# A list scheduler's two assumptions: half a microsecond more before TensorE's steps, and a later landing of short-row transfers

## The chip, the cores and the metric

The kernel runs on one core of one Trainium2 chip. The metric is the device time of one execution in microseconds (us). The engines are named as in the profile: PE is TensorE (PEld its weight loads), DVE is VectorE, ACT is ScalarE, POOL is GpSimd, SP is SyncE, which here only issues transfers.

## The reference, cut to what is computed

One layer of a hybrid backbone, in float32: 512 latent tokens and 256 context tokens of width 1024. A conditioning vector gives shifts, scales and gates; one wide projection feeds two groups of heads, a Mamba-2 scan (SSD) and a gated delta rule (GDN), each in both directions; then an output projection and an MLP of width 4096.

```python
p_lat = modulate(rmsnorm(x, norm1_g[l]), sh1, sc1) @ w_in[l]
p_ctx = modulate(rmsnorm(ctx, norm1_g[l]), sh1c, sc1c) @ w_in[l]
y_lat, y_ctx = token_mixers(p_lat, p_ctx, ...)      # convolutions, SSD scan, GDN scan, both directions
x = x + g1 * (y_lat @ w_out[l])
x = x + g2 * sq_relu_mlp(modulate(rmsnorm(x, norm2_g[l]), sh2, sc2), w_mlp1[l], w_mlp2[l])
...
# in gdn_scan, per chunk of 64 tokens and head:
tmat = eye + strictly_lower((k_beta k^T) * decay)
sol = triangular_solve(tmat, rhs, lower=True, unit_diagonal=True)
v_new = u_i - w_i S;   S_next = S * d_i + kd_i^T v_new;   o = qd_i S + qk_i v_new
```

The kernel inverts the triangular matrices in blocks of 128 tokens and applies the inverses in the scan.

## The kernel before, in words

Every large product is made of three PE passes over a high and a low part of both operands (`hH`, `hL`, `wH`, `wL`). The kernel runs in these stages:

- 0 to about 50 us: loads, norms and the modulation (`mp`, `xtp`), and the first weights.
- about 50 to 436 us: the projections of the items k, q, v, g, B, C, and the first x and z (`proj`, PSUM tiles `pl_*` of 512 latent columns and `pc_*` of 256 context columns, 24 passes each), each followed by a convolution on DVE (`conv`, tiles `cy_*`) and by transposes (`k3t`, `v4t` and the like). Among them run four inverses (`inverse(b)`, two heads each): `kk` and `qk` products, diagonal blocks sent to DRAM and back in another layout (`blkD` to `ND` and `YD`), a substitution on DVE (`TD`, `YD`, 60 steps), the result sent to DRAM (`invD`) and read back in blocks of 32 by 32 by 14 transfers of 48 KB with rows of 128 bytes (`X`, `Yf`, `Yb`), then small PE products (`z`, `x`, `y`, each with an ACT copy behind it), and the inverse is stored to `invF`.
- about 436 to 646 us: four scans (`scan(b)`: `ks`, `pp`, `up`, `op`), which begin by loading `Ys` from `invF`. The rest of the x and z projections and the SSD products (`st`, `yp`) lie between their steps.
- from about 680 us: output projection (`wo0a`, `wo1a`), then the MLP (`m1p`, `m2a`).

The order of instructions on each engine is not the order of the program text. `kernel()` traces the program once; `_plan` builds a graph of its instructions and dependencies (`_Graph`), gives each a cost (`_cost`), and runs an event simulation with a list of ready instructions for each engine (`run`). The order that comes out is then fixed for every engine, SP's transfers included, by `_keep`. At run time each engine follows its list strictly and waits at semaphores, so the plan's times count for nothing, but its order does.

Two places of the plan matter here. In `_cost`, a transfer occupies the queue for `gap` and lands `d` + 2000 ns after it; for an `X`, `Yf` or `Yb` load of 49,152 bytes this is 49152/150 = 328 ns of queue, and a landing 623 + 2000 = 2.6 us after that. Its issue occupies SP for 370 ns. In `run`, `finish` hands the result of instruction k to its user m on engine q:

```python
t = end + (50 if self.dma[k] else _LAT[e][q]) + _SLACK[q]
```

with `_SLACK = (0.0, 100.0, 100.0, 100.0, 0.0)`: a user on DVE, ACT or POOL gets 100 ns of margin, a user on PE (q = 0) gets none. Among ready instructions the one with the lowest `key` (mostly the place in the program text) goes first. A transfer is also held back while eight earlier ones have not landed in the plan (`_LANES`).

Of the kernel before, what the change touches and what calls it, by code (L numbers as in the profile page):

```python
# [1394 lines left out]
_WINDOW = 3413.4  # L1395
_SLACK = (0.0, 100.0, 100.0, 100.0, 0.0)
_LANES = 8
_MIX = 1.2e9
_STRETCH = 1.0

# [12 lines left out]
class _Graph:  # L1413
    def __init__(self, nc, tc, traced, ordered):
        kind = {i.name: type(i).__name__ for i in ordered}
        meta = {n for n, k in kind.items() if k.startswith("BassTile")}
        slots = {n for n in meta if kind[n] == "BassTileRelease"}
        self.ins = [i for i in traced if not kind[i.name].startswith("BassTile") and kind[i.name] != "InstRegisterMove"]
        self.at = {i.name: k for k, i in enumerate(self.ins)}
        psum, pool_of = set(), {}  # L1420
        for t in tc.tiles:
            if "PSUM" in str(t.space):
                psum.add(t.name)
        memo = {}

        def expand(n):
            if n not in memo:
                memo[n] = set()
                out = set()
                for a, _ in nc.dependency_edges(n):  # L1430
                    out |= expand(a) if a in meta else {a}
                memo[n] = out
            return memo[n]

        deps, sync, users = [], [], {}
        tiles = {t.name: t for t in tc.tiles}
        for k, i in enumerate(self.ins):
            d, s = set(), set()
            for a, info in nc.dependency_edges(i.name):
                if a in slots:  # L1440
                    continue
                if a in meta:
                    d |= expand(a)
                    s |= {x for x in expand(a) if kind[x] == "InstDMACopy"}
                else:
                    d.add(a)
                    if "NoSync" not in str(info.class_):
                        s.add(a)
            deps.append({self.at[a] for a in d if a in self.at})
            sync.append({self.at[a] for a in s if a in self.at})  # L1450
            for t in {_name(ap) for ap in list(i.outs) + list(i.ins)}:
                if t in tiles:
                    users.setdefault(t, []).append(k)
        opened = {}
        for i in traced:
            if kind[i.name] == "BassTilePoolBoundary" and "op=alloc" in str(i):
                pool = str(i).split("pool=")[1].split()[0]
                opened[pool] = {self.at[a] for a in expand(i.name) if a in self.at}
        tags = {}
        for t in tc.tiles:  # L1460
            if t.name in users:
                tags.setdefault(t.tag, []).append(t)
        for line in tags.values():
            bufs = line[0].tag_meta.bufs
            for k, t in enumerate(line):
                u = set(users[t.name])
                before = opened.get(t.mls.memorylocations[0].ant_tile_pool_name, set())
                if k >= bufs:
                    before = before | set(users[line[k - bufs].name])
                for n in users[t.name]:  # L1470
                    if not deps[n] & u:
                        deps[n] |= before
                        sync[n] |= {x for x in before if kind[self.ins[x].name] == "InstDMACopy"}
        n = len(self.ins)
        self.n, self.succ, self.need = n, [[] for _ in range(n)], [0] * n
        self.eng, self.dma, self.dur, self.gap = [], [], [], []
        self.table, self.accum, self.lock, self.shape = [], [], [], []
        for i in self.ins:
            e = _ENG.index(str(i.engine).split(".")[1])
            self.eng.append(e)  # L1480
            self.dma.append(kind[i.name] == "InstDMACopy")
            self._cost(i, e, kind[i.name], psum)
        for m in range(n):
            deps[m].discard(m)
            self.need[m] = len(deps[m])
            for d in deps[m]:
                same = self.eng[d] == self.eng[m] and not (self.dma[d] and d in sync[m])
                self.succ[d].append((m, same, d in sync[m]))

    def _cost(self, i, e, kind, psum):  # L1490
        table, accum, lock, shape = 0, False, False, 0
        w = _width(i.outs[0])
        gap = None
        if kind == "InstDMACopy":
            src = _name(i.ins[0])
            b = 4
            for q in i.outs[0].ap:
                b *= q[1]
            run = 4 * min(i.ins[0].ap[-1][1], i.outs[0].ap[-1][1])
            same = any(q[0] == 0 and q[1] > 1 for q in i.ins[0].ap)  # L1500
            gap = b / (380.0 if same else 400.0 if run >= 2048 else 320.0 if run >= 512 else 60.0 if src.startswith("in_") else 150.0)
            total = b / (300.0 if src.startswith("in_") else 140.0) + 600.0
            d = max(0.0, total - gap)
        elif e == 0:
            shape = tuple(i.tile_size)
            full = str(i.ins[0].dtype).endswith("float32") and str(i.ins[1].dtype).endswith("float32")
            if i.is_transpose:
                gap = max(84.0, 20 + 0.7 * w)
            elif not full:
                gap = 15 + 0.415 * w  # L1510
            elif shape == (32, 32):
                gap = 34.0
            elif shape[1] < 128:
                gap = 5 + 1.7 * w
            else:
                gap = max(218.0, 5 + 1.7 * w)
            d = gap + 163.0
            shape = (shape, tuple(i.tile_position or ()), full and not i.is_transpose)
        else:
            sp = [a for a in i.ins if hasattr(a, "memref") and _width(a) > 1]  # L1520
            ps = any(_name(a) in psum for a in sp)
            two = len(sp) > 1
            if e == 1:
                lock = not ps and kind != "InstMemset"
                if kind == "InstTensorTensor":
                    d = 145 + 1.04 * w
                elif kind == "InstReciprocal":
                    d = 150 + 6.2 * w
                elif kind == "InstTensorCopy":
                    d = 150 + (1.04 if ps or w >= 1024 else 0.55) * w  # L1530
                elif kind == "InstMemset":
                    d = 130 + 0.5 * w
                else:
                    d = 205 + 1.04 * w if two or ps else 140 + 0.6 * w
            elif e == 2:
                table = _TABLE.get(str(i.func).split(".")[-1], 0)
                accum = len(i.outs) > 1
                one = sum(hasattr(a, "memref") for a in i.ins) == 1
                d = (190 if one else 250) + 0.82 * w + (20 if ps else 0)
            else:  # L1540
                lock = True
                d = 250 + 2.0 * w if kind == "InstTensorTensor" else (130 if kind != "InstMemset" else 90) + 0.95 * w
        self.dur.append(d if e == 0 or gap is not None else d * _STRETCH)
        self.gap.append(gap)
        self.table.append(table)
        self.accum.append(accum)
        self.lock.append(lock)
        self.shape.append(shape)

    def run(self, key):  # L1550
# [15 lines left out]
        def finish(k, e, end, fr):  # L1566
            free[e] = fr
            heapq.heappush(events, (fr, 0, e))
            for m, same, sy in succ[k]:
                q = eng[m]  # L1570
                if same:
                    t = fr
                    if not self.dma[k] and e:
                        if self.dma[m]:
                            t = end + 28
                        elif sy:
                            t = end + (122 if self.accum[k] else 34)
                else:
                    t = end + (50 if self.dma[k] else _LAT[e][q]) + _SLACK[q]
                if t > ready[m]:  # L1580
                    ready[m] = t
                need[m] -= 1
# [5 lines left out]
        while done < n:  # L1588
# [15 lines left out]
            if not now[e]:  # L1604
                if soon[e]:
                    heapq.heappush(events, (soon[e][0][0], 0, e))
                continue
            p, k = heapq.heappop(now[e])
            if self.dma[k] and len(landed) >= _LANES and landed[-_LANES] > t:
                heapq.heappush(soon[e], (landed[-_LANES] + 30.0, p, k))  # L1610
                heapq.heappush(events, (t, 0, e))
# [73 lines left out]
def _plan(trace):  # L1685
# [12 lines left out]
    graph = _Graph(nc, tc, traced, ordered)  # L1698
    rank = graph.rank()
    key = [_MIX * k / graph.n - rank[k] for k in range(graph.n)]  # L1700
    _, order = graph.run(key)
    return [[graph.ins[k].name for k in line] for line in order]

# [41 lines left out]
```

## Time and profile before

| | us |
|---|---|
| median of 3 runs | 1163.1 (1160.6 to 1168.05) |
| profiled execution, its own time | 1160.29 |
| its span, first to last instruction | 1158.6 |
| PE busy | 1091.5 (94%) |
| DVE, ACT, POOL busy | 721.4, 604.0, 456.0 |

The profiled execution took 1160.29 us, 1.7 us more than its span and 2.8 us less than the median of the runs. PE's mean granted clock was 0.978 of full speed. Busy is the time in which an engine ran an instruction. In rows of busy time by stretch the engines stand in the order PE, PEld, DVE, ACT, POOL, each with its number of instructions, behind the stretch and its length. Idle time of an engine is put down to what released it last; "issue" stands where the profile shows no release.

### The profile page before, as it was taken

Reading aid. Unit: us, or ns where it says so; the run is one execution under the profiler, and the core shown is the slowest. Engines: PE = TensorE matmul, PEld = TensorE weight load, DVE = VectorE, ACT = ScalarE, POOL = GpSimd, SP = SyncE. Lnnn points to the kernel's source line nnn. Section 1 sums busy time; section 2 is a strip of 40 time slices with the busy share of each in tenths; the row PEclk is TensorE's granted clock in tenths of the full one; section 3 lists DMA queues with packets and bytes.
Section 4 is the critical chain, followed back from the end, with each engine's and each line's share of the span. In section 5 each row is a group of like instructions: output and inputs, shape, how many; then the busy total and the mean of one; then the engine's idle time right before and its main releaser. Section 6 shows DMA issues by size and latency. Waiting matters only on the chain.

```text
span 1158.6 us, 19228 instructions
## 1 busy us (share of the span) xinstructions
PE 1091.5 (94%) x7120; PEld 885.4 (76%) x7120; DVE 721.4 (62%) x1402; ACT 604.0 (52%) x1419; POOL 456.0 (39%) x386
## 2 busy tenths in 40 slices
PE   5799998998989999999999989999999999999997
PEld 2458877787868777788878868777777888888885
DVE  3775699897979557578766777878673022444023
ACT  4647656648364577578886674125333122444133
POOL 1216444442331332222322254433545445555462
PEclk9899999999999999999999989998999999999999
DMA  9577746686564694745372277743443333333332
GB/s 313 182 198 200 229 146 185 195 227 170 157 163 146 154 347 104 267 123 207 103 273 73 92 282 237 227 136 100 137 146 109 92 107 93 91 103 98 91 104 96
DMA packets 189334, 188.44 MB, mean 163 GB/s; under 512 B 41548, under 2 KB 140153, under 8 KB 189241
## 3 DMA queue, kind: packets, MB, share of 16 engines
q1 hardware_dynamic: 188336, 186.04, 52.6%
q8 instruction: 56, 0.92, 0.3%
q10 hardware_dynamic: 905, 1.18, 0.3%
q14 instruction: 37, 0.30, 0.1%
HBM read 151.45 MB, written 35.73 MB: 162 GB/s over the span
## 4 chain that ended last, share of the span: by engine, by line
PE 70%; DVE 11%; ACT 8%; DMA 6%; issue 3%; SPq 1%; POOL 0%; ACTq 0%; DVEq 0%; POOLq 0%
PE m1p L62 15%; PE m2a L62 15%; PE wo0a L62 4%; PE wo1a L62 3%; PE pl_x L62 3%; PE pl_v L62 3%; PE pl_g L62 2%; PE yp L62 2%; PE op L62 2%; PE pc_v L62 2%; DMA st_q<-in_w_in_dram 2%; PE pp L62 2%; PE pl_z L62 2%; PE up L62 2%; PE pc_x L62 2%
## 5 line engine op out<-in xcount | busy, mean ns | idle before, releaser
L77 POOL TENSOR_TENSOR wL_m<-st_m,wH_m 128x512 fp32r<-128x512 f32 x128 | 177.4, 1405 | 186.6 <-ACT wH_m L68 177.1
L68 ACT ACTIVATE wH_m<-st_m 128x512 fp32r<-128x512 f32 x128 | 77.1, 625 | 187.0 <-PE m2a L62 111.0
L62 PE MATMUL m1p<-h2hL,wH_m 128*128 128x512 f32 (+1 forms) x272 | 104.5, 384 | 1.6 <-DVE h2hL L77 1.5
L62 PE MATMUL m1p<-h2hH,wH_m 128*128 128x512 f32 (+1 forms) x272 | 103.6, 383 | 2.5 <-ACT rl L68 2.0
L62 PE MATMUL m1p<-h2hH,wL_m 128*128 128x512 f32 (+1 forms) x272 | 103.1, 380 | 0.0
L62 PE MATMUL m2a<-wL_m,aH 128*128 128x512 f32 x256 | 99.4, 389 | 0.0
L62 PE MATMUL m2a<-wH_m,aL 128*128 128x512 f32 x256 | 99.4, 389 | 0.0
L62 PE MATMUL m2a<-wH_m,aH 128*128 128x512 f32 x256 | 98.9, 389 | 0.0
L77 DVE TENSOR_TENSOR rtmp<-m2a,g2r 128x512 f32<-128x512 f32 x16 | 10.7, 683 | 140.1 <-PE m2a L62 140.0
L77 DVE TENSOR_TENSOR rl<-rl 128x512 f32<-128x512 f32 x32 | 47.5, 1484 | 51.8 <-ACT rl L68 51.5
L62 PEld LDWEIGHTS m1p<-h2hH,wH_m 128*128 128x128 f32 x272 | 51.8, 191 | 14.0 <-ACT rl L68 4.0
L77 POOL TENSOR_TENSOR wL_wo<-st_wo,wH_wo 128x512 fp32r<-128x512 f32 x32 | 45.2, 1433 | 41.1 <-ACT wH_wo L68 35.4
L74 DVE SCALAR_TENSOR_TENSOR macc<-mw,sil,macc 128x256 f32<-128x256 f32 x84 | 56.4, 671 | 7.2 <-DMA mw<-in_w_mod_dram 5.4
L62 PEld LDWEIGHTS m1p<-h2hL,wH_m 128*128 128x128 f32 x272 | 52.1, 191 | 11.5 <-DVE h2hL L77 2.4
L77 DVE TENSOR_TENSOR TD<-YD,ND 112x30 f32<-112x30 f32 (+14 forms) x120 | 59.6, 497 | 0.9
L62 PEld LDWEIGHTS m1p<-h2hH,wL_m 128*128 128x128 f32 x272 | 52.2, 192 | 9.4
L62 PEld LDWEIGHTS m2a<-wH_m,aH 128*128 128x128 f32 x256 | 48.0, 188 | 10.1
L62 PEld LDWEIGHTS m2a<-wL_m,aH 128*128 128x128 f32 x256 | 48.0, 188 | 10.0
L62 PEld LDWEIGHTS m2a<-wH_m,aL 128*128 128x128 f32 x256 | 48.0, 188 | 9.9
L77 DVE TENSOR_TENSOR YD<-YD,TD 112x30 f32<-112x30 f32 (+14 forms) x120 | 54.5, 454 | 0.9
L665 POOL TENSOR_SCALAR_AFFINE_SELECT rw<-rw 128x512 f32<-128x512 f32 x32 | 24.0, 764 | 64.7 <-ACT er L68 60.6
L68 ACT ACTIVATE wH_wo<-st_wo 128x512 fp32r<-128x512 f32 x32 | 18.5, 623 | 50.0 <-PE wo0a L62 21.6
(496 smaller groups left out, 3224.2 us busy)
## 6 DMA issues: line engine op xcount, KB each, us to landing
st_m<-in_w_mlp_dram SPq DMA_DIRECT2D x64, 512.0 KB
wm<-in_w_mod_dram SPq DMA_DIRECT2D x16, 512.0 KB
rw<-rowsD SPq DMA_DIRECT2D x16, 512.0 KB
st_wo<-in_w_out_dram SPq DMA_DIRECT2D x16, 512.0 KB
mw<-in_w_mod_dram SPq DMA_DIRECT2D x16, 512.0 KB
Ys<-invF SPq DMA_DIRECT2D x8, 768.0 KB
st_k<-in_w_in_dram SPq DMA_DIRECT2D x8, 512.0 KB
st_g<-in_w_in_dram SPq DMA_DIRECT2D x8, 512.0 KB
```

The lines of the kernel that those rows point to most:

```text
L62: PE.matmul(o, lhsT=lhsT, rhs=rhs, start=start, stop=stop)
L68: ACT.activation(out=o, in_=i, func=f, **kw)
L74: (eng or DVE).scalar_tensor_tensor(out=o, in0=a, scalar=s, in1=b, op0=op0, op1=op1)
L77: (eng or DVE).tensor_tensor(out=o, in0=a, in1=b, op=op)
L665: POOL.affine_select(out=rw[:, d_], in_=rw[:, d_], pattern=[[0, n], [pat, P]], compare_op=ALU.is_ge, fill=NEG, base=0, channel_multiplier=cm_)
```

## The change

Two constants of the plan become active. `_EARLY = 500.0`: for every user on PE that stands in the program text before the first load of `Ys` (index `self.scans`), a result of another engine or a transfer counts as ready 500 ns later. `_SHORT = 2500.0`: a transfer that does not read an input of the kernel, and whose contiguous run is below 512 bytes, lands 2.5 us later in the plan. These are the four writes of `blkD` and the 14 loads of `X`, `Yf` and `Yb` of each inverse, and the two small `mod2` loads in the tail. The loads of `ND` and `YD` have long rows and keep their cost. The other three constants are 0 and change nothing. No instruction is added or removed and no cost on the chip changes; what changes is the order in each engine's list, everywhere behind the first choice that falls out another way.

```diff
+_SHORT = 2500.0
+_FROM = 0.0
+_EARLY = 500.0
+_LATE = 0
+_NEAR = 0.0
...
+        self.scans = min(k for k, i in enumerate(self.ins) if _name(i.outs[0]).startswith("Ys"))
...
-            d = max(0.0, total - gap)
+            d = max(0.0, total - gap) + (0.0 if src.startswith("in_") else _SHORT if run < 512 else _FROM)
...
                     t = end + (50 if self.dma[k] else _LAT[e][q]) + _SLACK[q]
+                    if q == 0 and m < self.scans:
+                        t += _EARLY
...
             p, k = heapq.heappop(now[e])
+            if e == 0 and shape and self.shape[k][0] != shape[0] and _NEAR:
...
+    rows = [k for k in range(graph.n) if graph.dma[k] and _name(graph.ins[k].ins[0]) == "in_w_mod_dram"]
+    for k in rows[24:40]:
+        key[k] += _LATE * _MIX / graph.n
```

## Rows read from the trace of the kernel before

**Rows 1.** The page, part 1: busy us (share of the span) xinstructions.

```profile
PE 1091.5 (94%) x7120; PEld 885.4 (76%) x7120; DVE 721.4 (62%) x1402; ACT 604.0 (52%) x1419; POOL 456.0 (39%) x386
```

**Rows 2.** Busy time by stretch, five engines; then PE clock, DMA share, GB/s.

```profile
0.00:50.00 50.00, 31.86 (x217) 15.81 (x218) 24.83 (x56) 27.53 (x45) 9.22 (x26) 0.90 0.74 250
50.00:436.00 386.00, 359.78 (x3170) 296.57 (x3169) 299.41 (x615) 228.68 (x535) 146.85 (x133) 0.97 0.67 194
436.00:700.00 264.00, 253.84 (x1750) 211.13 (x1750) 186.47 (x451) 195.81 (x566) 80.73 (x69) 0.99 0.50 168
700.00:1158.60 458.60, 446.04 (x1988) 361.92 (x1986) 210.68 (x283) 151.96 (x275) 219.22 (x158) 0.99 0.41 124
...
900.00:1000.00 100.00, 100.00 (x443) 82.81 (x442) 21.02 (x23) 25.73 (x45) 49.13 (x37) 1.00 0.34 100
```

**Rows 3.** Waits of PE, 50 to 436 us: total us, times, longest us.

```profile
PE y L62 <- issue: 7.0, 4, 3.8
PE z L62 <- DMA X<-invD: 4.4, 2, 2.4
PE pc_k L62 <- DVE cy_k L74: 2.6, 1, 2.6
PE k3t L65 <- DVE kT L74: 2.5, 1, 2.5
PE v4t L65 <- DVE vT L74: 1.7, 1, 1.7
PE kk L62 <- DVE At L74: 1.4, 1, 1.4
...
PE pl_v L62 <- POOL wL_v L77: 0.2, 1, 0.2
PE k1t L65 <- DVE kT L74: 0.2, 1, 0.2
```

**Rows 4.** Timeline of PE around three waits: start us, us, instruction, [idle before].

```profile
150.02 0.88 PE L65 MATMUL k3t<-ident,kT 128*128 128x128 f32 x6 [2.51 <-DVE kT L74]
150.65 0.67 PE L62 MATMUL pl_g<-hL,wH_g 128*128 128x512 f32 x1
...
272.40 0.25 PE L62 MATMUL z<-X,At 32*32 32x32 f32 x4 [2.40 <-DMA X<-invD]
272.58 0.50 PE L62 MATMUL pl_v<-hH,wH_v 128*128 128x512 f32 x1
...
395.89 0.25 PE L62 MATMUL z<-X,At 32*32 32x32 f32 x4 [2.01 <-DMA X<-invD]
396.07 0.38 PE L62 MATMUL pc_x<-hH,wL_x 128*128 128x256 f32 x1
```

**Rows 5.** Busy time in the stretches that follow four waits (columns as rows 2).

```profile
150.80:154.20 3.40, 3.40 (x10) 2.63 (x10) 3.40 (x5) 3.30 (x15) 3.00 (x3) 0.50 0.34 121
273.70:277.10 3.40, 3.40 (x17) 3.23 (x16) 3.37 (x9) 2.82 (x9) 0.00 (x0) 0.50 0.83 227
341.90:348.80 6.90, 5.82 (x59) 4.56 (x61) 2.25 (x6) 3.42 (x7) 0.00 (x0) 0.51 0.18 61
396.50:399.90 3.40, 3.40 (x18) 3.11 (x17) 0.70 (x1) 0.00 (x0) 0.00 (x0) 0.51 0.51 83
```

**Rows 6.** Timeline of SP's queue: loads of two inverses.

```profile
264.82 6.43 SPq L90 DMA_DIRECT2D X<-invD  x6
...
272.32 0.47 SPq L90 DMA_DIRECT2D Yf<-invD  x1
...
390.61 4.83 SPq L90 DMA_DIRECT2D X<-invD  x6
```

**Rows 7.** Timeline of PE: the longest wait put down to issue.

```profile
342.98 0.26 PE L62 MATMUL y<-Yf,Z 32*32 32x32 f32 x1 [3.79 <-issue]
```

**Rows 8.** DMA queues, 339 to 344 us: packets, MB, share of 16 engines.

```profile
q8 instruction: 1, 0.02, 1.3%
```

**Rows 9.** Instructions by tile: ns min/median/max, first and last start.

```profile
L62 PE MATMUL pp<-r,Ys x160: 270/275/377, 444.4 to 645.2; 128*128 128x128 f32 x160
L62 PE MATMUL pl_z<-hH,wH_z x64: 388/395/483, 417.9 to 676.2; 128*128 128x512 f32 x64
L62 PE MATMUL yp<-rw,xt x128: 272/273/421, 424.3 to 690.2; 128*64 128x128 f32 x128
```

**Rows 10.** Busy time in the stretch behind the last scan (columns as rows 2).

```profile
650.00:690.00 40.00, 35.23 (x218) 27.76 (x216) 30.37 (x49) 30.47 (x71) 17.94 (x14) 0.92 0.63 215
```

More of the change, by code (lines that the diff above doesn't have):

```diff
@@ L1608, in run @@
             p, k = heapq.heappop(now[e])
+            if e == 0 and shape and self.shape[k][0] != shape[0] and _NEAR:
+                for q, m in heapq.nsmallest(12, now[0]):
+                    if self.shape[m][0] == shape[0] and q < p + _NEAR:
+                        now[0].remove((q, m))
+                        now[0].append((p, k))
+                        heapq.heapify(now[0])
+                        p, k = q, m
+                        break
             if self.dma[k] and len(landed) >= _LANES and landed[-_LANES] > t:
```

## The prediction

> **What bounds the kernel now.** I read the busy times first: PE works 94% of the span, and no other engine passes 62% [rows 1]. So PE's time is the kernel's time, and what an order can give is the time in which PE stands idle or runs at its lower clock. The stretches say where that is [rows 2]. Up to 50 us PE is idle for 18.1 us; there the first inputs arrive and nothing else can be done. From 700 us on it is idle for 12.6 us of 458.6. From 436 to 700 us, in the scans, 10.2 us. Between 50 and 436 us it is 386.0 - 359.78 = 26.2 us, and the mean granted clock there is 0.97, about 0.03 x 386 = 11.6 us more, worked out from a rounded figure. These 38 us are all that the change can win in the stretch for which it is made. DVE works 299 of the 386 us there, so it is no bound, but late results of DVE are common.
>
> The waits of that stretch come next [rows 3]. There are 17 rows. The largest is the small product y of the inverses, with no release shown: 7.0 us in four waits. Next is z, which waits for the X loads: 4.4 us in two. The other 15 rows sum to 14.7 us; they are single waits for another engine or a transfer, from 2.6 down to 0.2 us, and in 11 of them the wait is 0.5 us or more.
>
> Then I looked at what stands behind such a wait in PE's list [rows 4]. Behind z at 272.40 us comes a pl_v product which needs nothing from z and runs at once, behind z at 395.89 a pc_x product, behind k3t at 150.02 a run of pl_g products. PE had work, but its list put a product whose input was late in front of it. That kind of wait can be cured by order. The wait of pc_k is another kind: its one PSUM buffer was still being read by DVE, and what follows in the list is more pc_k.
>
> Last, the clock [rows 5]. After three of these waits PE runs 3.4 us at a granted clock of 0.50 (0.51 once), which is 1.2 GHz in place of 2.4. Where PE has work without a break, as it does in the stretches at 273.7, 396.5 and 150.8 us, this loses half of the stretch: 1.7 us each.
>
> **The change part by part.** No instruction is added or removed, so every term is a wait that goes, comes or moves.
>
> *The landing of short rows, with the half microsecond.* The plan issues six X loads in 6 x 0.37 = 2.2 us and has them land 2.6 us after their place in the queue. On the chip the six issues took 6.43 us in one inverse and 4.83 us in another [rows 6], 4.2 and 2.6 us more than planned. So what is late is mostly the issuing; the change pays for it in the landing, which serves z just as well. z is now planned 2.5 + 0.5 = 3.0 us later, more than either wait (2.40 and 2.01), and pl_v or pc_x goes in front. I take both waits as gone, 4.4 us, and the two stretches at half clock behind them, 3.4 us: -7.8 us. Bounds: 0, if z gets late elsewhere by as much, and -7.8. In the other two inverses z does not wait, so there the margin is not needed; it costs nothing while PE has projections to run.
>
> *The half microsecond for all other PE steps.* In the 15 rows it can take at most 0.5 us of each of 11 waits and the whole of four smaller ones (0.4, 0.3, 0.2, 0.2): 6.6 us. It can't where nothing stands ready (pc_k, and the first waits below 80 us). I take half: -3.3 us. Bounds: 0, and -6.6 with the stretch at 150.8 us back at full clock, 1.7, so -8.3.
>
> *The y waits.* The largest, 3.79 us at 342.98 [rows 7], has no engine's release behind it; in that window the queue of instruction loads moved one packet of 0.02 MB [rows 8]. All four y waits stand in runs of the inverses' small products, which use up instructions faster than wide ones, and I read them as PE waiting for its own instructions. Neither assumption speaks of that. Spreading the small products among wide ones would help, closing them up would hurt, and the diff decides neither: 0. Bounds: -7.0 and, for the 6.9 us at a clock of 0.51 behind the longest, -3.4, so -10.4; on the other side four more such waits at the same mean of 1.75 us, with 1.7 us of half clock each: +13.8.
>
> The Trainium skill, in "Runtime: NRT & Kernel Launch", section "Instruction fetch mechanics", states that instructions are refilled in blocks of 16 KiB and that crossing a block is mostly hidden. By that rule the y waits would have another cause and the bound of +13.8 would fall away; the sum would stay. The trace speaks against "hidden" here: 3.79 us with only that load to see.
>
> *Later inverses.* Each inverse's blkD writes and its loads land 2.5 us later in the plan, and its chain enters PE some six times from another engine, 0.5 us each: 2.5 + 2.5 + 3.0 = 8 us an inverse in the plan. SP issues ND and YD behind the blkD writes; with a later landing other transfers, weight loads among them, get in front, and ND's users on ACT and DVE (the substitution) come later. If the inverses come later, so do the Ys loads and the scans. What hides this is the work that belongs to no scan: the last pp of the scans starts at 645.2, but pl_z runs to 676.2 and yp to 690.2 [rows 9], and between 650 and 690 us PE is busy for 35.2 us with it [rows 10]. Work pulled forward as filler leaves that much for the scans' gaps. So a delay up to about 30 us costs nothing, and I take 0. Without this cover each microsecond of a later scan costs one.
>
> *Weight loads and the tail.* The plan holds a transfer back while eight have not landed; 14 loads that land later hold SP's list longer, so weight loads may be planned behind them. PE waited only 0.2 us for a weight's low part in the whole stretch [rows 3]; ten times that is my upper bound, so 0 to +2 us. The mod2 loads move by 2.5 us in a tail where PE waits little: 0.
>
> *New waits.* Every list changes behind the first different choice. Some products now stand in front whose inputs come late by the same lateness of DVE. Bounds from the nearest rows: with the present idle share of 436 to 700 us, 3.9%, the 386 us would hold 15 us of idle time, which would be 11 us less; with its own share, 6.8%, nothing is won. Part of this is counted above; I take +2 us for it and for the weights.
>
> The sum: -7.8 - 3.3 + 2 = -9.1 us. The profiled execution took 1160.3 us, so it would take 1151.2; the median stands 2.8 us above it, so I forecast 1154.
>
> In "Perfetto Trace Analysis", section "Identifying the Most-Contended Engine", the Trainium skill says that weight-load busy time is a better measure of PE's distance to its limit than matmul busy time. By that rule the 50 to 436 us stretch would have 386 - 297 = 89 us to win. The trace narrows this: from 900 to 1000 us PE has no gap and its weight loads are busy 82.81 of 100 us [rows 2]; 296.57/0.828 is 358 us, so the idle 26.2 us is indeed what is left.
>
> **The rivals.** *Larger gain.* Besides the X waits the y waits shrink too, as z, x and y are mixed with more projections, and the half-clock stretches go with them. For it: three of the waits shown brought 1.7 us of half clock with them, so gains can come in pairs. Against it: nothing in the diff aims at instruction loads. At its end it gives -7.8 - 8.3 - 10.4 = -26.5 us, 1137; I put it from 1137 to 1149.
>
> *The waits only change places* (the change doesn't do what it says). DVE's lateness is not a constant: waits of 2.5, 1.7 and 1.4 us stand where half a microsecond of air would leave 2.0, 1.2 and 0.9, and if SP still issues slowly, y waits for Yf and Yb where z waited for X. For it: these loads come right behind X in SP's list, with an issue of 0.47 us [rows 6]. Then the X gain of 7.8 us goes and 1159 to 1167 remains, likeliest 1162.
>
> *Slower, by instruction loads.* The air lets the small products of an inverse become ready in larger groups, and PE runs through them faster than its instructions arrive. Its place is the z, x, y chain of each inverse, its price 1.75 us a wait and 1.7 us of half clock. It decides from about four more such waits: +13.8, less the 3.3 us of the other steps, with the X gain lost among them, is +10.5, so 1174 (1167 to 1183).
>
> **How the numbers follow.** Forecast, 1149 to 1159: 0.48. Larger gain: 0.22. Waits change places: 0.18. Slower: 0.12. About 1% (11.6 us) is what a measurement of this kernel can tell from no change. Faster by more than that, below 1151.5: 0.22 and a quarter of 0.48, together 0.34. Slower, above 1174.7: half of 0.12, 0.06. Within: 0.60. The range goes from 1141, which leaves out a third of the larger gain (0.07), to 1167, which leaves out the slower case (0.12).
>
> **What the profile would show.** If the X step is right, z starts without a wait on X in all four inverses, with pl or pc products in front of it, and the clock stays at full there. If the half microsecond works, the 15 small rows between 50 and 436 us sum to about 11 us. If the y step is right, some 7 us put down to issue remain. If the cover holds, pp starts later than 444 us or not, while the idle time from 436 to 700 us stays near 10 us. Idle time from 50 to 436 us should fall from 26 to about 20 us and the half-clock time by two stretches. I would be wrong if instruction waits vanish or multiply, or if the scans run out of filler.

## The result, and the profile after

The changed kernel takes 1174.2 us (median of 6 runs, 1171.0 to 1177.4) against 1162.9 us before (6 runs): a ratio of 1.0096, interval 1.0067 to 1.0124. Forecast were 1154 us and a range of 1141 to 1167. The profiled execution took 1170.97 us, 10.7 us more than that of before; its span is 10.6 us longer.

Busy time by stretch of the changed kernel, columns as in [rows 2]. The stretch from 436 to 700 us is cut at 640 us:

```profile
0.00:50.00 50.00, 32.63 (x232) 17.66 (x233) 26.46 (x58) 28.20 (x46) 9.20 (x26) 0.97 0.75 250
50.00:436.00 386.00, 356.35 (x3114) 292.03 (x3113) 291.54 (x609) 226.87 (x531) 146.40 (x133) 0.96 0.64 180
436.00:640.00 204.00, 201.98 (x1428) 170.55 (x1427) 145.33 (x365) 153.76 (x459) 64.19 (x54) 1.00 0.57 193
640.00:740.00 100.00, 88.83 (x493) 71.63 (x492) 66.94 (x123) 51.20 (x121) 35.06 (x26) 0.95 0.55 184
740.00:1169.20 429.20, 415.07 (x1860) 338.01 (x1858) 183.95 (x251) 141.82 (x260) 205.18 (x148) 0.99 0.38 113
```

The same of the kernel before, where it is cut otherwise than in [rows 2]:

```profile
436.00:640.00 204.00, 199.24 (x1410) 166.88 (x1410) 142.83 (x375) 154.32 (x465) 55.88 (x50) 1.00 0.50 166
640.00:740.00 100.00, 94.59 (x516) 75.52 (x515) 77.12 (x125) 54.05 (x120) 43.33 (x34) 0.97 0.64 213
740.00:1158.60 418.60, 406.04 (x1816) 330.66 (x1814) 177.19 (x235) 139.39 (x256) 200.75 (x145) 0.99 0.37 110
```

Up to 640 us PE is busy for 32.63 + 356.35 + 201.98 = 590.96 us after and 31.86 + 359.78 + 199.24 = 590.88 us before. The stretch for which the change is made wins nothing; it has 3.4 us more idle time, which two further executions of the list of before have nearly as well (28.9 and 29.3 us idle instead of 26.2, the kernels with a late scan below, whose lists are those of before up to 412 us). By 640 us both kernels have put the same time into PE. Then, in 100 us, PE is idle for 11.2 us instead of 5.4, and its clock is 0.95 instead of 0.97, some 2 us more. Behind 740 us another 1.6 us are idle. That is 9.4 of the 10.6 us; the last 1.2 I can't place.

Instructions of the scans and of the SSD work, by tile, in the changed kernel (ns min/median/max, first and last start), and the line of before for the scans' first products:

```profile
L62 PE MATMUL pp<-vtr,Ys x32: 270/275/377, 449.6 to 619.8; 128*128 128x128 f32 x32
L62 PE MATMUL pp<-r,Ys x160: 270/275/377, 457.7 to 662.4; 128*128 128x128 f32 x160
L62 PE MATMUL pl_z<-hH,wH_z x64: 387/397/500, 421.7 to 679.6; 128*128 128x512 f32 x64
L62 PE MATMUL yp<-rw,xt x128: 272/273/421, 428.3 to 690.6; 128*64 128x128 f32 x128
```

```profile
L62 PE MATMUL pp<-vtr,Ys x32: 270/275/283, 436.4 to 607.4; 128*128 128x128 f32 x32
```

The scans begin 13.2 us later (449.6, not 436.4) and their last product 17.2 us later (662.4, not 645.2). The other work moves less: the last pl_z 3.4 us later (679.6, not 676.2), the last yp 0.4 us (690.6, not 690.2) [rows 9]. So work that should lie behind the scans has been done beside them.

The first product of the output projection, wo0a, comes behind the last scan; it starts at 696.2 us, before at 679.5 (the changed kernel first, then the kernel before):

```profile
L62 PE MATMUL wo0a<-wH_wo,yhH x32: 389/389/774, 696.2 to 721.8; 128*128 128x512 f32 x32
L62 PE MATMUL wo0a<-wH_wo,yhH x32: 389/389/628, 679.5 to 712.7; 128*128 128x512 f32 x32
```

Between the last pp and that product, in the same order:

```profile
662.40:696.20 33.80, 23.70 (x153) 19.14 (x152) 22.40 (x41) 27.41 (x72) 16.25 (x13) 0.92 0.53 187
```

```profile
645.20:679.50 34.30, 31.87 (x204) 25.48 (x202) 25.41 (x46) 26.53 (x69) 13.63 (x12) 1.00 0.57 193
```

The way from the last pp to wo0a is about 34 us in both. Before, PE had work in it for 31.87 us; now for 23.70, at a granted clock of 0.92. What it waits for there is shown by the timeline of PE in the changed kernel:

```profile
672.71 0.84 PE L65 MATMUL x7t<-ident,cy_x 128*128 128x128 f32 x6 [1.14 <-DVE cy_x L74]
...
682.84 1.30 PE L62 MATMUL st<-xw,Bt 128*64 128x128 f32 x16 [1.63 <-POOL xw L77]
...
686.87 0.44 PE L62 MATMUL yp<-rw,xt 128*64 128x128 f32 x4 [2.72 <-issue]
...
694.93 1.44 PE L62 MATMUL sstat<-onesg,sqa 128*128 128x1 f32 x6 [3.65 <-POOL sqa L77]
```

From 682.84 on these are the steps of the last SSD item. They wait for another engine, one of them for no release that the profile shows (issue), and no wide projection is left to lie between them. Before, the output projection itself lay there: wo0a began 10.7 us ahead of the last yp; now it begins 5.6 us behind it.

PE's waits from 50 to 436 us, to be set beside [rows 3]:

```profile
PE y L62 <- issue: 3.3, 3, 1.7
PE k3t L65 <- DVE kT L74: 3.2, 1, 3.2
PE pl_k L62 <- DVE cy_q L74: 2.9, 1, 2.9
PE kk L62 <- DVE At L74: 2.8, 2, 1.5
...
PE x L62 <- issue: 1.5, 1, 1.5
...
PE yp L62 <- issue: 0.9, 1, 0.9
```

The wait for the X loads is gone. The waits put down to issue are 5.8 us (7.0 before). All others, for another engine or transfer, sum to 23.8 us; before they were 14.8. (Such sums are taken before rounding; the prediction's 14.7 is the sum of the rounded rows.)

SP's queue at the last inverse's end, in the changed kernel:

```profile
422.26 1.83 SPq L90 DMA_DIRECT2D invF<-Yb  x1
433.72 1.09 SPq L90 DMA_DIRECT2D rw<-rowsD  x2
434.91 0.42 SPq L90 DMA_DIRECT2D st_x<-in_w_in_dram  x1
435.38 1.33 SPq L90 DMA_DIRECT2D Ys<-invF  x1
```

The last store of the inverse goes out at 422.3 us and the first load of Ys at 435.4: SP's list has two row loads in front, which waited for their buffer. This was a suspect of its own.

### The profile page after: what moved, and what is told of

Same layout as the page of the kernel before. It is cut to its first block, busy times and chain, and to the rows that moved or that the text cites. A ratio compares the mean times of both kernels' runs of the same rounds, so it can differ in the third digit from the quotient of the medians.

```text
span 1169.2 us, 19247 instructions
## 1 busy us (share of the span) xinstructions
PE 1094.9 (94%) x7120; PEld 889.9 (76%) x7120; DVE 714.2 (61%) x1402; ACT 601.9 (51%) x1417; POOL 460.0 (39%) x386
## 4 chain that ended last, share of the span: by engine, by line
PE 71%; DMA 9%; DVE 7%; ACT 6%; issue 4%; POOL 2%; SPq 1%; POOLq 0%; ACTq 0%; DVEq 0%
PE m1p L62 15%; PE m2a L62 15%; PE pl_v L62 4%; PE wo1a L62 3%; PE pl_x L62 3%; PE pl_g L62 3%; PE op L62 2%; PE yp L62 2%; PE pl_k L62 2%; PE pp L62 2%; PE pc_x L62 2%; PE pc_v L62 2%; DMA wm<-in_w_mod_dram 2%; PE pl_q L62 2%; PE pl_z L62 2%
## 5 line engine op out<-in xcount | busy, mean ns | idle before, releaser
L77 DVE TENSOR_TENSOR rtmp<-m2a,g2r 128x512 f32<-128x512 f32 x16 | 10.7, 683 | 140.1 <-PE m2a L62 140.1
L77 DVE TENSOR_TENSOR TD<-YD,ND 112x30 f32<-112x30 f32 (+14 forms) x120 | 54.0, 450 | 1.3
L77 POOL TENSOR_TENSOR wL_x<-st_x,wH_x 128x512 fp32r<-128x512 f32 x16 | 20.3, 1292 | 83.3 <-ACT wH_x L68 41.8
L68 ACT ACTIVATE wH_wo<-st_wo 128x512 fp32r<-128x512 f32 x32 | 18.3, 623 | 53.4 <-PE wo0a L62 21.7
```

Source lines behind the costliest of these rows:

```text
L68: ACT.activation(out=o, in_=i, func=f, **kw)
L77: (eng or DVE).tensor_tensor(out=o, in0=a, in1=b, op=op)
```

## The experiments

"Air" below is the half microsecond of `_EARLY`. The theory (A): half a microsecond at each hop of the inverses' chain makes the last inverse late in the plan, PE's list puts other work in front of the scans, and that work is missing behind them, where nothing else covers the last steps. Its rival (B): a late scan is covered, as predicted, and the loss comes from the order before the scans. A third (C): each touch of the constants draws another list, and lists scatter.

All runs beside runs of the kernel before on the same chip. "First pp" and "last pp" are the first and last scan products with Ys, "others" PE's waits from 50 to 436 us apart from issue and X, all from the profiled execution of each; the three sorts of wait together are, within 0.3 us, PE's idle time in that stretch. The last column is PE's idle time from 640 to 740 us. The profiled executions of "landing, inverses preferred" (1162.8 us) and "landing only, 1.25 us" (1162.2) took 5 to 6 us more than the medians of these kernels.

| kernel | ratio to before (interval) | first pp, us | last pp, us | X waits | issue waits | others | idle 640-740 |
|---|---|---|---|---|---|---|---|
| before | 1 | 436.4 | 645.2 | 4.4 | 7.0 | 14.8 | 5.4 |
| changed | 1.0096 (1.0067 to 1.0124) | 449.6 | 662.4 | 0 | 5.8 | 23.8 | 11.2 |
| scan late by 20 | 1.0097 (1.0067 to 1.0127) | 459.0 | 672.3 | 3.7 | 7.0 | 18.4 | 9.6 |
| scan late by 10 | 1.0039 (1.0017 to 1.0060) | 445.8 | 655.5 | 3.2 | 7.4 | 18.3 | 5.5 |
| last inverse spared | 1.0002 (0.9979 to 1.0024) | 436.9 | 650.1 | 0.2 | 5.5 | 21.4 | 5.5 |
| half microsecond only | 1.0107 (1.0075 to 1.0139) | 448.6 | 663.4 | 0.6 | 16.9 | 16.8 | 10.0 |
| landing only | 0.9960 (0.9940 to 0.9981) | 433.5 | 646.7 | 0 | 4.3 | 21.9 | 4.5 |
| Ys first on SP | 1.0076 (1.0039 to 1.0113) | 447.3 | 661.4 | 0 | 5.7 | 23.6 | 10.9 |
| 20 ns | 1.0026 (1.0002 to 1.0049) | 442.8 | 655.8 | 4.2 | 8.2 | 15.6 | 6.8 |
| landing, inverses preferred | 0.9966 (0.9942 to 0.9990) | 432.7 | 645.8 | 0 | 4.1 | 21.7 | 7.7 |
| air on inverses' products only | 1.0106 (1.0064 to 1.0148) | 449.8 | 665.1 | 1.3 | 8.5 | 24.6 | 12.8 |
| air on all but these | 1.0015 (0.9990 to 1.0040) | 441.0 | 653.9 | 0 | 6.9 | 18.8 | 6.4 |
| landing only, 4.0 us | 1.0077 (1.0053 to 1.0101) | 446.4 | 664.9 | 0 | 2.0 | 27.1 | 9.1 |
| landing only, 1.25 us | 0.9954 (0.9931 to 0.9977) | 436.7 | 653.4 | 0.3 | 5.6 | 17.2 | 5.6 |

**A late scan by itself.** The kernel before, in which only the plan's time for the first Ys loads is moved. PE's list is the same as before up to the first scan product.

```diff
+        self.late = {k for k, i in enumerate(self.ins) if _name(i.outs[0]).startswith("Ys0_")}
...
+                if m in self.late:
+                    t += 20000.0
```

> The kernel before, with one thing changed in the plan: the loads of the first scan's Ys count as ready 20 us later. Up to the first scan product the list of PE is the same as before. Theory A (the loss of the changed kernel comes from its scans, which begin 13 us later; work left behind the last scan does not cover that): first scan product at about 450 to 456 us, not 436; the idle time of PE up to 436 us stays within 2 us of before, the idle time between 640 and 720 us grows by 5 us or more, and the time goes up by 7 to 14 us, to 1170 to 1177. Theory B (the prediction's: up to 30 us of other work covers a late scan; the loss comes from the order before the scans, with more changes between wide and small products): within 3 us of before.

It took 1173.2 us against 1162.2. A late scan alone costs as much as the whole change, so B's cover of 30 us does not hold. The busy time by stretch of this kernel:

```profile
0.00:50.00 50.00, 32.77 (x222) 16.82 (x223) 25.46 (x57) 28.37 (x46) 9.20 (x26) 0.90 0.74 251
50.00:436.00 386.00, 356.71 (x3141) 292.54 (x3141) 299.07 (x611) 227.96 (x533) 146.35 (x133) 0.97 0.66 190
436.00:640.00 204.00, 195.85 (x1370) 162.88 (x1364) 146.67 (x354) 149.88 (x445) 62.52 (x54) 0.98 0.53 175
640.00:740.00 100.00, 90.38 (x522) 72.47 (x522) 65.65 (x128) 54.31 (x132) 30.47 (x23) 0.97 0.51 173
```

The place is not wholly as I expected. From 640 to 740 us PE is busy for 4.2 us less than before; that is the end of the scans, as in the changed kernel, though less than the 5 us asked for. But 3.4 us are lost between 436 and 640: yp waits once for 5.9 us, where SSD steps were pulled in front of the first scan. And the first 436 us, with the same list, differ by 2.2 us of busy time from one execution to the other. Only 4.2 us lie where A puts them, so it is in part chance that the total equals that of the change.

The same with `10000.0`:

> As the run with 20 us, but the loads of the first Ys count as ready only 10 us later; up to the first scan product PE's list is that of before. If a late scan costs from the first microsecond on, first scan product at 446 to 450 us and half the cost of 20 us, +4 to +7 us, 1166 to 1169. If there is a cover that is used up first, the cost is within 3 us of before, 1159 to 1165, and the cover lies between some 10 and 20 us.

It took 1166.5 us against 1161.7, at the low end of what a cost from the first microsecond on would give. The profile says otherwise about the place:

```profile
436.00:640.00 204.00, 196.35 (x1365) 164.43 (x1364) 140.16 (x358) 148.21 (x443) 52.65 (x46) 0.97 0.51 172
640.00:740.00 100.00, 94.49 (x534) 75.62 (x534) 77.59 (x132) 59.31 (x140) 44.82 (x35) 0.97 0.60 198
```

From 640 to 740 us PE is as busy as before, 94.49 against 94.59 us, although the last pp came 10.3 us later. So the cover at the scans' end exists and holds some 10 us; with 17.2 us, in the changed kernel, it is used up. The cost of this kernel lies at the scans' begin, where yp waits once for 4.4 us. One more thing can be read from the two kernels with a late scan: with PE's list of before, "others" are 18.3 and 18.4 us, not 14.8, so a difference of some 4 us in that column can be the scatter between executions.

**The last inverse spared.** The changed kernel, with both assumptions only up to the third inverse's store. (The later landing is taken from the last inverse's loads; its four blkD writes keep it.)

```diff
+        self.last = [k for k, i in enumerate(self.ins) if _name(i.outs[0]).startswith("invF")][5]
+        for k in range(self.last, n):
+            if self.dma[k] and _name(self.ins[k].ins[0]).startswith("invD"):
+                self.dur[k] -= _SHORT
...
-                    if q == 0 and m < self.scans:
+                    if q == 0 and m < self.last:
```

> The changed kernel, in which neither assumption holds for the last inverse (half a microsecond and later landing only up to the third inverse's store). Theory A: the last inverse and the scans come earlier than in the changed kernel, first scan product at 440 to 446 us against 449.6, and the time falls by 3 to 8 us, to 1166 to 1171. Theory B: the order up to there is the changed one, so the time stays within 3 us of the changed kernel, 1171 to 1177. If a scan's begin has nothing to do with it and the time is only the luck of one list, it can fall anywhere in 1160 to 1177.

It took 1163.5 us against 1162.2: all of the loss is gone, 2.5 us beyond what was expected, with the first pp at 436.9 us, 3 us earlier than expected. The three inverses in front keep the changed costs, so these were not the loss. "Others" is 21.4 us here too, nearly that of the changed kernel, without costing anything measurable against before: the X waits are gone instead, and the idle time of the stretch is 27.3 us.

**Each half alone.** `_SHORT = 0.0` and `_EARLY = 500.0`:

> Only the half microsecond before PE's steps, landing as before. Theory A: the inverses come a little later through their four to six hops, the scans begin 3 to 8 us later than before, the time goes up by 0 to 5 us, 1163 to 1168. Theory B: the half microsecond is what mixes the products anew, so this alone gives most of the loss, 1169 to 1175. The X waits of PE (4.4 us) should stay at 3 us or more, as the landing is not changed.

1174.0 us against 1162.2, as much as both together; A had expected 1163 to 1168, so its size for this half was wrong; B's 1169 to 1175 fits. X waits fell to 0.6 us without the later landing, also against the expectation: z's own half microsecond suffices. The profile shows two places. The last pp is at 663.4 and PE idle from 640 to 740 us for 10.0 us, 4.6 more than before; and from 50 to 436 us it is idle for 34.6 us, 8.4 more, with waits of another kind in front:

```profile
PE z L62 <- issue: 6.9, 1, 6.9
PE y L62 <- issue: 6.5, 2, 3.5
PE pc_x L62 <- issue: 3.5, 1, 3.5
```

16.9 us are put down to issue, against 7.0 before. This is the price of the rival "slower, by instruction loads", which the changed kernel itself (5.8 us) does not show.

`_SHORT = 2500.0` and `_EARLY = 0.0`:

> Only the later landing of short rows, no half microsecond. The X waits of PE should fall from 4.4 us to under 1 us, as 2.5 us is more than either of them. Theory A: each inverse comes later by up to 5 us, the scans begin 5 to 10 us later than before, the time goes up by 2 to 7 us, 1165 to 1170. Theory B: few products change places before the scans, so the X waits and the half clock behind them are won and the time falls by 3 to 8 us, to 1155 to 1160.

1157.1 us against 1162.2, faster than both kernels. The X waits are gone; the scans begin at 433.5, not later as A had it, so a later landing of 2.5 us alone does not move them. A's number (+2 to +7) was wrong here, B's (-3 to -8) right. But PE's idle time from 50 to 436 us is 26.5 us, as before (26.2): other waits stand where the X waits stood (21.9 us). What fell in this profile is PE's busy time, 1084.1 us of the span instead of 1091.5, at a mean granted clock of 0.985 instead of 0.978.

**Is it the transfers on SP?** The changed kernel, with two entries of SP's list moved:

```diff
+    ys = [k for k in order[4] if out(k).startswith("Ys0_")]
+    rest = [k for k in order[4] if k not in ys]
+    at = 1 + max(j for j, k in enumerate(rest) if out(k).startswith("invF"))
+    order[4] = rest[:at] + ys + rest[at:]
```

> The changed kernel, with the two loads of the first scan's Ys put on SP's list right behind the last inverse's store, in front of two row loads and a weight load that held SP for 11 us there; every other list is the changed kernel's. If PE's list sets the scan's begin (PE waited only 0.3 us for its first scan product at 449.6 us), the loads are issued at about 424 us, the first scan product stays within 2 us of 449.6 and the time within 3 us of the changed kernel, 1171 to 1177. If the transfers stuck on SP are what makes the scans late, the first scan product comes at 440 to 445 us and the time falls by 5 us or more, to 1169 or less.

The Ys loads went out at 421.7 us, 13.7 us earlier; the first pp came 2.3 us earlier and the time is 1170.9 us, both a hair outside the first branch and some 2 us short of the second. PE's list holds the scans back more than the Ys loads do: in the changed kernel PE waited only 0.3 us for its first pp. The scan's other loads (vtr, kTs) still stood behind the row loads, from 433.4 us on; moving these too was not tried.

**Scatter.** `_SHORT = 0.0` and `_EARLY = 20.0`:

> The kernel before with 20 ns in place of 500 ns before PE's steps and no later landing: a change too small to stand for a mechanism, which still draws another list. If the loss of the half microsecond is a mechanism (later inverses, later scans), this stays within 5 us of before, 1157 to 1167, with the first scan product within 4 us of 436. If lists scatter by 10 us at the smallest touch, it can lie at 1170 or more, and the loss of the change would say nothing about air.

1165.5 us against 1161.7, interval 1.0002 to 1.0049, with the first pp 6 us later, where at most 4 were expected. So a touch without meaning moves the time by some 0.3%. A difference of 1% is more than that, one of 0.3% may be the list alone.

**An earlier scan.** The later landing alone, and everything that Ys depends on preferred by 100 places (`seen` is the set of the Ys loads and all they depend on):

```diff
+    for k in seen:
+        key[k] -= 100.0 * _MIX / graph.n
```

> Only the later landing, and besides all steps that the first scan's Ys loads depend on are preferred by 100 places of the program's order, so that the inverses and the scans come earlier. If an earlier scan gives what a later one costs, the first scan product comes at 425 to 432 us and the time falls below that of the later landing alone, 1150 to 1155. If the tail is then bound by the SSD chain behind the scans, it stays within 3 us of it, 1154 to 1160; new waits from projections that come later could also take it to 1165.

1156.8 us, the same as the later landing alone; the scans began only 0.8 us earlier. It does not tell what an early scan would give.

**Whose air is it?** The changed kernel, with the half microsecond kept for the products `z1_`, `x1_`, `y1_`, `z2_`, `y2_`, `kk`, `qk` (`self.inverse`), or taken from them:

```diff
-                    if q == 0 and m < self.scans:
+                    if q == 0 and m < self.scans and m in self.inverse:
```

> The changed kernel with the half microsecond kept only for the inverses' own products (kk, qk, z, x, y) and taken from the projections, transposes and all other steps. If the loss comes from air in the inverses' chain, which moves the scans in PE's list, the first scan product stays at 445 to 452 us and the time at 1168 to 1176. If the air of the projections is what costs, the time falls to that of the later landing alone, 1154 to 1160, and the first scan product to 432 to 438 us.

1175.6 us against 1163.2; first pp at 449.8 us. The loss comes with the air of the inverses' own products. It doesn't lie only at the scans' end: PE is idle for 12.8 us from 640 to 740, 7.4 more than before, and for 34.6 us from 50 to 436, 8.4 more, as with the half microsecond alone. The other way round (`not in`):

> The changed kernel with the half microsecond taken from the inverses' own products and kept for the projections, transposes and all other steps before the scans. If air in the inverses' chain is the loss, the first scan product comes at 433 to 442 us and the time at 1155 to 1163. If air in the projections is the loss, it stays at 1168 to 1176. If half a microsecond does what it was meant for, PE's waits for DVE, ACT and POOL between 50 and 436 us fall below the 14.7 us of before; if waits only change places, they stay at 18 us or more.

1164.4 us against 1163.2, with an interval that holds 1; first pp at 441.0. And the wins for which this half was predicted don't come: others are 18.8 us, no less than the 14.8 to 18.4 us of the list of before.

**More and less landing.** `_EARLY = 0.0` with `_SHORT = 4000.0`, then 1250.0:

> Only the later landing, 4.0 us in place of 2.5. The X waits stay under 1 us, as with 2.5. If a late scan costs, the first scan product comes 4 to 10 us later than with 2.5 (at 437 to 444 us) and the time rises by 2 to 8 us over it, to 1159 to 1165. If the margin costs nothing, the time stays within 3 us of it, 1154 to 1160.

> Only the later landing, 1.25 us in place of 2.5. If the X waits go by the margin, 1 to 2.5 us of the 4.4 us remain, and the time lies between before and the 2.5 us, 1157 to 1162. If the gain of 2.5 us was the luck of its list, this may lie on either side, 1155 to 1168, with X waits of any size.

With 4.0 us: 1172.2 us against 1163.2, a first pp at 446.4 and a last one at 664.9. The time came out 7 us above what was expected and the scan 2.4 us later than expected: this constant too makes the scans late when it is large enough. With 1.25 us: 1156.9 us against 1163.2, as good as 2.5 us, and the X waits are 0.3 us although the margin is shorter than the waits were (2.40 and 2.01 us). So the gain doesn't scale with the margin; I take it that it is enough for z to go behind the projection at hand.

Over all rows of the table: with a last pp up to 654 us the ratio lies between 0.995 and 1.002, at 655 to 656 between 1.003 and 1.004, and from 661 us on between 1.0076 and 1.0107, whichever edit made the scans late. The last pp also comes later by whatever PE lost ahead of it, so this alone is no proof; but the six slow kernels share the place as well. They are idle for 9.1 to 12.8 us from 640 to 740 us, the other eight for 4.5 to 7.7. And in these six the first wo0a starts behind all yp products, in the other eight at least 3.7 us ahead of the last: in the slow kernels the SSD work is used up before the output projection begins.

## Why the prediction was wrong

The step that failed is "later inverses": a delay of the scans up to about 30 us was priced at nothing, because PE had 35.2 us of other work behind the last scan [rows 10]. The amount was nearly right (3.5 of the 35.2 us are wo0a's own first products, from 679.5 us on) and the use wrong. That work is what PE's list takes when the scans are late, and it is then no longer there at the end. In the changed kernel its last yp starts at the same time as before, while the way from the last pp to wo0a is 34 us as before, so PE stands in that gap with 8.2 us less work. The cover holds about 10 us of delay (run with 10 us: 94.49 of 100 us busy), not 30. This is the last of the prediction's own signs of being wrong, "if the scans run out of filler"; the number it named for the cover, about 10 us idle from 436 to 700 us, came out at 12.1 and would have hidden it, as 2.8 us less idle time up to 640 us stand against the loss behind it. The price of 8 us an inverse in the plan was a fair size: the last y product starts 9.8 us later (421.0, not 411.2), and the list adds 3.4 us before the first pp.

*The X loads*: right as a mechanism. Both waits are gone, in the changed kernel and with the landing alone; there the time falls by 5.1 us, of the 7.8 us in the sum. How much of that the waits gave is open: the sum had 4.4 us for them, and the idle time of the stretch did not fall (26.5 us); the lower busy time at a higher clock is the part that the profile shows. So the rival "the waits only change places" was right about the waits and wrong about the time. That less margin does it too (1.25 us) is something I had not seen: z had a ready projection directly behind it, and I read it so that any margin that lets one pass takes the rest with it.

*The half microsecond for the other steps*: no such gain. The sum had -3.3 us. The other waits are 23.8 us in the changed kernel, 16.8 with the half microsecond alone and 18.8 with air on the projections, against 14.8 to 18.4 with the list of before. The rise goes with the later landing, which alone has 21.9. That every new list puts other late products in front, so that an offset does not absorb DVE's lateness, fits this but was not tested. *New waits* were priced at +2 us with a bound that turned on idle shares; the waits show +9, while the whole idle time of the stretch grew by 3.4. But this is not what the change lost: the kernel with the last inverse spared has +6.6 us of such waits and no loss.

*The y waits*: priced at 0; they went from 7.0 to 5.8 us with x and yp counted in, so right for this kernel. The rival "slower, by instruction loads" gave 1174, the measured time, by luck: its mechanism, more waits for instructions, is not at work in the changed kernel. It is in the half microsecond alone: 16.9 us. Its chance of 0.12 should have been that of a late scan, which I had as a term without cost instead of as a rival.

*Weight loads and tail*: the row loads in front of Ys on SP are such a case (11 us), but moving Ys in front of them won nothing clear of noise (ratio 1.0076, interval to 1.0113, against 1.0096). In the tail behind 740 us 1.6 us were lost, h2p waiting 3.4 us for ACT; not pursued.

What stays open: how the loss of the half microsecond alone, and of air on the inverses' products only, divides between the waits ahead of the scans and the late scans, whether the half microsecond won anything at all, and how much of each difference of 0.3% is the list.

## What to carry to other kernels

Work that fills gaps is spent once: if a list takes it earlier because a chain starts later, look at the chain's far end, where it is missing, before calling a delay covered. A margin in a scheduler's cost is no measure of safety: put on every hop it adds up along the longest chain, so give it to the one transfer that is known to be late. On the steps off that chain it cost nothing clear of noise here, and won nothing. And a fixed order redrawn by a meaningless constant moves the time by 0.3% here, so a gain of that size needs a stretch of the profile that shows it.

## What the runs showed of the hardware

PE waits for its own instructions in runs of small products, and for longer than I had priced. In the kernel with the half microsecond alone, PE stood for 6.9 us, with nothing to wait for that the profile names, while weights and data moved at 244 GB/s; the busy time of that stretch (columns as in [rows 2]) and the product behind it:

```profile
279.50:286.40 6.90, 0.04 (x1) 0.10 (x1) 3.21 (x10) 1.41 (x4) 0.00 (x0) 0.72 0.93 244
```

```profile
286.45 0.80 PE L62 MATMUL z<-X,At 64*64 64x64 f32 x11 [6.91 <-issue]
```

From 283.5 to 285.5 us the queue of instruction loads moved one packet; PE went on within 1 us of that window. In the kernel before, the packet of the longest such wait [rows 7] lies between 340 and 342 us, and PE went on at 342.98. That the load waited behind a busy DMA (share 0.93 here, 0.88 there from 339.2 to 343.0) is argued from these two, not shown. That the waits go with such a packet is regular: in the 14 kernels, 46 waits from 50 to 436 us of 0.7 us or more are put down to issue, and before 44 of them, all but two of yp, a packet of 16 KB of that queue has landed 1.3 to 1.65 us before PE goes on. The Trainium skill, "Runtime: NRT & Kernel Launch", section "Instruction fetch mechanics", calls the crossing of an instruction block mostly hidden; these waits are not, 2.0 to 16.9 us of them in the stretch from 50 to 436 us, depending on the list.
